# 48 constant products ahead of two projections of a hybrid decoder trunk

## The chip, the cores and the metric

The kernel runs on one core of a Trainium2 chip. The metric is the device time of one execution in microseconds (us). The engines are TensorE (PE, its weight loads PEld), VectorE (DVE), ScalarE (ACT), GpSimd (POOL) and SyncE (SP), which here only issues DMAs. Each engine works through its own queue in order and waits at the head of it on semaphores.

## The reference, cut to what matters

Two layers over 512 tokens of width 1024, float32. Layer 0 is a gated DeltaNet: one input projection gives queries, keys, values, a gate and two small sets of logits; a short causal convolution and SiLU follow; a delta rule in chunks runs over 16 value heads; a gated norm and an output projection end it. Layer 1 is a gated short convolution of width 2048.

```python
for i in range(DEPTH):
    h = rms_norm(x, pre_norm_w[i])
    if i % 2 == 0: y = gated_deltanet_mixer(h, ...)   # (h @ w_in) -> conv, SiLU, delta rule -> @ w_out
    else:          y = short_conv_mixer(h, ...)        # (h @ w_in) -> conv, gates -> @ w_out
    x = x + rms_norm(y, post_norm_w[i])
```

The change touches only TensorE's work around the first input projections of layer 0. Nothing that it computes goes into the result.

## The kernel before, in words

**Projections.** A projection of 128 output columns is a "unit": 1024 inputs are 8 blocks of 128, and each block takes three products of 128x128 by 128x512 in a float32 of reduced precision (`mm3`, lines 184 to 187: high by high, high by low, low by high). So a unit is 24 products into one PSUM bank. `unit` (line 189) first calls `weights` (line 172), which loads 512 KB of raw weights into `wraw`, casts them to a high part (line 167, on GpSimd for these units) and subtracts for the low part (line 168, on VectorE). `n_w` counts these calls. The high and low parts have two buffers each; once a tile `w3` exists, each call whose number divides by three puts its parts there instead (line 178, named `w` in the trace).

**Banks.** The units' banks come from the pool `ps_p`, which has two, both under the tag `pp`. A unit can begin when the unit two before it has been read out of its bank. For the first units of the kernel the read is one VectorE product with the row scales: line 363 (`start_keys`) for the four units of the start, which `start_unit` (line 868) emits, line 486 for the next four, which come from `in_unit` (line 479).

**The start.** The four units of the start are key 0, key 1, query 0 and query 1 of head group 0 (the first is computed beside the logits). Then come keys 0 and 1 and queries 0 and 1 of group 1: the calls of `unit` with `n_w` 1, 2, 3 and 4. In between stand small pieces of other work on TensorE. `norms` (line 540) transposes a key or query (tile `tok`) for ScalarE to square and sum (line 548, tile `junk`); `c_est` (line 561) follows it with the Gram products of a key (`kk`, line 583), the scaling of decay tables on ScalarE (line 597), and the products into `E` on VectorE (line 598). The triangular solve of a group (`c_solve`, line 611) starts from `E`: ScalarE copies at line 638, then a long run of small VectorE instructions at lines 645 and 647.

**What `w3` waits for.** `decay_tables` (line 422) for group 1 loads a table `gb` of 1 MB, applies 16 exponentials on ScalarE (line 449) and stores it by one DMA (line 454, `dt_d<-gb`). The tile `w3` has the same memory (tag `E3`, line 462), so the parts of the unit with `n_w` 3 can only be written when that DMA has read the table.

**Also at this time** the normed input is made for all later units: `start_h` (line 876) computes `hf` on VectorE (line 879) for 8 blocks, and splits each into `hh` (ScalarE, line 167) and `hl` (VectorE, line 168).

**What sets the order.** TensorE's order is that of the program text; other work is woven in by a counter of TensorE time that the text keeps itself (`pump.now`, advanced by `pump.pe`). VectorE's, ScalarE's and GpSimd's order is written out only up to line 890 (`start.close()`). After that, and for the DMA queue always, a planner in the compiler sets the order: it runs the program through a timeline of its own (line 38) and on each engine takes, of what is ready at that time, the instruction of the best priority. Priorities come from `pump.now` with an offset (`at`, line 149); weights and key norms have early ones, `start_h` late ones. So the planned order depends on when, in the planner's timeline, TensorE delivers.

**Constants.** `ones` (line 133) is a 128x128 float32 tile of ones. Fourteen products of it by itself stand at the very beginning (line 301).

Of the kernel before, what the change touches and what calls it, by code (L numbers as in the profile page):

```python
# [18 lines left out]
P = 128  # L19
# [41 lines left out]
}  # L61


class Pump:
# [46 lines left out]
def trunk_kernel(ctx, tc, xT, x, cols, rows, eye, post0, pre1, post1, w_in, w_out, sw_in, sw_out, out):  # L111
    nc = tc.nc
# [20 lines left out]
    ones = cst.tile([P, P], F32, name="ones")  # L133
# [3 lines left out]
                            fill=0.0, base=0, channel_multiplier=-1)  # L137
# [24 lines left out]
    def pd(shape, name):  # L162
        return ps_d.tile(shape, F32, tag="pd", name=name)
# [6 lines left out]
    third, n_w = [], [0]  # L170

    def weights(src, hi_eng=None, store=None):
# [8 lines left out]
        split(hi, lo, raw, hi_eng)  # L181
        return hi, lo

    def mm3(ps, lh, ll, rh, rl, start, stop):
        nc.tensor.matmul(ps, lhsT=lh, rhs=rh, start=start, stop=False)  # L185
        nc.tensor.matmul(ps, lhsT=lh, rhs=rl, start=False, stop=False)  # L186
        nc.tensor.matmul(ps, lhsT=ll, rhs=rh, start=False, stop=stop)  # L187

    def unit(src, rhs, t=slice(0, T), hi_eng=None):


        K, m, n = len(rhs), src.shape[2], t.stop - t.start
        with at(-20):
            hi, lo = weights(src, hi_eng)
        ps = ps_p.tile([P, n], F32, tag="pp", name="pp")
        for k in range(K):
            mm3(ps[:m], hi[:, k], lo[:, k], rhs[k][0][:, t], rhs[k][1][:, t], k == 0, k == K - 1)
            pump.pe(3 * MM * n / T)
        return ps
# [49 lines left out]
    with ExitStack() as L0:  # L249
# [33 lines left out]
        start = ExitStack()  # L283
# [253 lines left out]
                nc.scalar.activation(gs.zT[:, a], ps, AF.Silu)  # L537
            gs.nz += 1

        def norms(tl, ss):  # L540

            junk = dl.tile([P, P], F32, tag="junk", name="junk", bufs=1)
            tok = pd([P, NC, P], "tok")
            for c in range(NC):
                nc.tensor.transpose(out=tok[:, c], in_=tl[:, c * P:(c + 1) * P], identity=ident)
            pump.pe(0.43, False)
            for c in range(NC):
                last_sq = nc.scalar.activation(junk, tok[:, c], AF.Square, accum_out=ss[:, c:c + 1])
            nc.vector.tensor_scalar_add(ss, ss, EPS)
            return tok, last_sq  # L550

        def c_qnorm(gs, kh):
            while len(gs.kT) < 2 or gs.est <= kh:
                yield 0.5
            yield (15,)
            ss = sm.tile([P, NC], F32, tag="ssq", name="ssq")
            norms(gs.qT[kh], ss)
            nc.vector.tensor_scalar_mul(gs.epsa[:, kh], ss, EPS * P)
            gs.nq += 1

        def c_est(gs, kh):
            g = gs.g
            while not gates_done or (g > 1 and not groups[g - 2].done):
                yield 1
            kT = gs.kT[kh]
            if kh == 0:
                gs.nrm = dl.tile([P, 6, NC], F32, tag="nrm", name="nrm")[:, :2]
                gs.epsa = dl.tile([P, 2, NC], F32, tag="epsa", name="epsa")
                gs.bp, gs.bpe = (dl.tile([P, 4, NC], F32, tag=n, name=n) for n in ("bp", "bpe"))
                gs.E = dl.tile([P, 16, P], F32, tag="E", name="E", bufs=2)  # L570
            yield (11 if g else 4,)
            ss = sm.tile([P, NC], F32, tag="ssn", name="ssn")
            tok, last_sq = norms(kT, ss)
            ktok = dl.tile([P, NC, P], F32, tag="ktok", name="ktok", bufs=4)
            kte = 0 if g == 0 else 1
            if kte == 1:
                nc.scalar.copy(ktok, tok)
            gs.ktok[kh] = ktok
            normed_k.append(1)
            kk = pd([P, NC, P], "kk")  # L580
            for c in range(NC):
                s = slice(c * P, (c + 1) * P)
                nc.tensor.matmul(kk[:, c], lhsT=kT[:, s], rhs=kT[:, s], start=True, stop=True)
            pump.pe(0.9, False)
            rk2 = sm.tile([P, 1, NC], F32, tag="rk2", name="rk2")
            nc.vector.reciprocal(rk2[:, 0], ss)
            h2, g2 = slice(2 * kh, 2 * kh + 2), slice(4 * g + 2 * kh, 4 * g + 2 * kh + 2)
            nc.vector.tensor_tensor(out=gs.bp[:, h2], in0=beta[:, g2], in1=rk2.to_broadcast([P, 2, NC]), op=ALU.mult)
            for r in range(2):
                hl_, h = 2 * kh + r, 4 * g + 2 * kh + r  # L590
                if g == 0:
                    dt = dt0[h]
                else:
                    dt = es.tile([P, NC, P], F32, tag="dt", name="dt")
                    nc.sync.dma_start(out=dt, in_=dt_d[h])
                for c in range(NC):
                    nc.scalar.activation(dt[:, c], dt[:, c], AF.Copy, scale=gs.bp[:, hl_, c:c + 1])
                last_e = nc.vector.tensor_tensor(out=gs.E[:, 4 * hl_:4 * hl_ + 4], in0=kk, in1=dt, op=ALU.mult)
                nc.sync.dma_start(out=dt_d[h], in_=dt)
            if kte == 0:  # L600
                nc.vector.tensor_copy(ktok, tok)
            if g == 0:
                fence[:] = last_e, last_sq
            nc.vector.tensor_tensor(out=gs.bpe[:, h2], in0=gs.bp[:, h2], in1=edec[:, g2], op=ALU.mult)
            rk = rsqrt(sm, ss, [P, NC], "rk")
            nc.gpsimd.tensor_tensor(out=gs.nrm[:, kh], in0=ss, in1=rk, op=ALU.mult)  # L606
            gs.est += 1
            if gs.est == 2:
                pump.add(c_solve(gs))
# [193 lines left out]
        def c_gate(gs, c, po):  # L803

            g = gs.g
            s = slice(c * P, (c + 1) * P)
            junk = dl.tile([P, P], F32, tag="junk", name="junk", bufs=1)
            so = dl.tile([P, 4], F32, tag="so", name="so")
            for a in range(4):
                nc.scalar.activation(junk, po[:, a], AF.Square, accum_out=so[:, a:a + 1])  # L810
            fy = dl.tile([P, 4], F32, tag="fy", name="fy")
            nc.vector.scalar_tensor_tensor(out=fy.rearrange("p (k r) -> p k r", r=2),
                                           in0=so.rearrange("p (k r) -> p k r", r=2), scalar=1.0 / P,
                                           in1=gs.epsa[:, :, c:c + 1].to_broadcast([P, 2, 2]),
                                           op0=ALU.mult, op1=ALU.add)
            f = rsqrt(dl, fy, [P, 4], "f")
            while gs.nz < 4:
                yield 1
            of = dl.tile([P, 4, P], F32, tag="d3", name="of", bufs=2)
            for a in range(4):  # L820
                nc.scalar.activation(of[:, a], po[:, a], AF.Copy, scale=f[:, a:a + 1])
            po_live[0] -= 1
            yield (12,)
            pt = pd([P, 4, P], "pot")
            for a in range(4):
                nc.tensor.transpose(out=pt[:, a], in_=of[:, a], identity=ident)
            pump.pe(0.43, False)
            og = dl.tile([P, 4, P], F32, tag="d3", name="og", bufs=2)
            nc.vector.scalar_tensor_tensor(out=og, in0=pt, scalar=ccol(C_NW), in1=gs.zT[:, :, s],
                                           op0=ALU.mult, op1=ALU.mult)  # L830
            if g < 3:
                oh = dl.tile([P, 4, P], F32R, tag="d3", name="ohs", bufs=2)
                split(oh, og.bitcast(F32R), og)
                nc.sync.dma_start(out=og_d[0, g, :, :, s], in_=oh.bitcast(F32))
                nc.sync.dma_start(out=og_d[1, g, :, :, s], in_=og)
            else:
                if c == 0:
                    gs.oh = dl.tile([P, 4, T], F32R, tag="E", name="oh3", bufs=2)
                    gs.ol = dl.tile([P, 4, T], F32R, tag="zT", name="ol3")
                split(gs.oh[:, :, s], gs.ol[:, :, s], og)  # L840
            gs.ngate += 1
# [25 lines left out]

        def start_unit(w, kh, q, hooks={}):
            ps = ps_p.tile([P, T], F32, tag="pp", name="pp")
            for k in range(KD):  # L870
                mm3(ps, w[0][:, k], w[1][:, k], *xop[k], k == 0, k == KD - 1)
                pump.pe(3 * MM)
                hooks.get(k, lambda: None)()
            u_kq(first, kh, q, start_keys(ps))
# [58 lines left out]
        def out_products(h0, cs, n, hi_eng):  # L933

            banks = [ps_p.tile([P, 512], F32, tag="pp", name="pa") for _ in cs]
            for kk in range(4):
                with at(-16):
                    hi, lo = weights(w_out_v[:, h0 + 2 * kk:h0 + 2 * kk + 2, wide[n]], hi_eng)
# [250 lines left out]
```

## Time and profile before

| | us |
|---|---|
| time, median of 3 runs | 1017.25 |
| lowest and highest | 1015.12, 1018.17 |
| time of the profiled execution | 1017.51 |
| its span, first to last instruction | 1015.6 |
| TensorE busy within the span | 960.8 |
| VectorE, ScalarE, GpSimd busy | 611.7, 420.1, 239.6 |
| mean granted TensorE clock, share of full | 0.976 |

Times in the rows below count from the span's start. A row of the timeline gives start, length, engine, line, operation and tiles (output, then inputs), a count, and in brackets the idle time of the engine before it with what ended that. Matmul lengths are modelled and overlap, so the pace of a run is the distance between starts. A float32 product of `ones` leaves two matmul records. The granted clock is 1.00 at 2.4 GHz and 0.50 at 1.2 GHz.

### The profile page before, as it was taken

Reading aid. Unit: us, or ns where it says so; the run is one execution under the profiler, and the core shown is the slowest. Engines: PE = TensorE matmul, PEld = TensorE weight load, DVE = VectorE, ACT = ScalarE, POOL = GpSimd, SP = SyncE. Lnnn points to the kernel's source line nnn. Section 1 sums busy time; section 2 is a strip of 40 time slices with the busy share of each in tenths; the row PEclk is TensorE's granted clock in tenths of the full one; section 3 lists DMA queues with packets and bytes.
Section 4 is the critical chain, followed back from the end, with each engine's and each line's share of the span. In section 5 each row is a group of like instructions: output and inputs, shape, how many; then the busy total and the mean of one; then the engine's idle time right before and its main releaser. Section 6 shows DMA issues by size and latency. Waiting matters only on the chain.

```text
span 1015.6 us, 14732 instructions
## 1 busy us (share of the span) xinstructions
PE 960.8 (95%) x5430; PEld 805.5 (79%) x5430; DVE 611.7 (60%) x1100; ACT 420.1 (41%) x1002; POOL 239.6 (24%) x446
## 2 busy tenths in 40 slices
PE   7965989998999999999998899999999999999997
PEld 4854768886888788887876899888888888888886
DVE  8578998845996794735469976443344343342233
ACT  4576665535645644334212554233232233222123
POOL 6253731335235423416634000000000000000001
PEclk9886999999999999999999899999999999999999
DMA  6233763246334621793645566433333333323322
GB/s 195 70 110 125 228 199 116 62 137 175 104 88 152 179 81 53 225 354 126 206 135 178 150 174 181 131 93 104 93 94 104 94 93 104 94 92 104 97 91 83
DMA packets 172391, 133.91 MB, mean 132 GB/s; under 512 B 6272, under 2 KB 146176, under 8 KB 171936
## 3 DMA queue, kind: packets, MB, share of 16 engines
q1 hardware_dynamic: 172176, 132.88, 43.2%
q8 instruction: 43, 0.70, 0.3%
q14 instruction: 28, 0.23, 0.1%
q10 hardware_dynamic: 144, 0.09, 0.0%
HBM read 117.16 MB, written 15.79 MB: 131 GB/s over the span
## 4 chain that ended last, share of the span: by engine, by line
PE 70%; DVE 13%; DMA 7%; ACT 4%; issue 3%; POOL 3%; SPq 0%; POOLq 0%; DVEq 0%; ACTq 0%
PE pp L185 16%; PE pp L187 16%; PE pp L186 16%; PE pf L185 2%; PE pf L187 2%; PE pf L186 2%; DVE tm L645 2%; DVE wlo L168 2%; DMA eg<-gt_d 2%; DVE Na L647 2%; PE pa L186 1%; PE pa L187 1%; DMA gb<-gt_d 1%; PE pa L185 1%; PE u L759 1%
## 5 line engine op out<-in xcount | busy, mean ns | idle before, releaser
L185 PE MATMUL pp<-hh,whi 128*128 128x512 f32 (+1 forms) x624 | 236.7, 379 | 4.5 <-DVE acc L471 2.2
L186 PE MATMUL pp<-hl,whi 128*128 128x512 f32 (+1 forms) x624 | 231.0, 370 | 1.0 <-DVE r L988 1.0
L187 PE MATMUL pp<-hh,wlo 128*128 128x512 f32 (+1 forms) x624 | 231.0, 370 | 0.0
L168 DVE TENSOR_TENSOR wlo<-wraw,whi 128x1024 fp32r<-128x1024 f32 x115 | 141.8, 1233 | 134.0 <-ACT whi L167 107.3
L167 ACT CAST whi<-wraw 128x1024 fp32r<-128x1024 f32 x64 | 67.4, 1052 | 185.2 <-PE pp L186 107.4
L185 PEld LDWEIGHTS pp<-hh,whi 128*128 128x128 f32 x624 | 119.1, 191 | 24.2 <-POOL nrm L606 2.6
L187 PEld LDWEIGHTS pp<-hh,wlo 128*128 128x128 f32 x624 | 119.0, 191 | 20.0
L186 PEld LDWEIGHTS pp<-hl,whi 128*128 128x128 f32 x624 | 119.2, 191 | 19.0 <-DVE hl L168 1.2
L185 PE MATMUL pp<-hh,w 128*128 128x512 f32 (+1 forms) x304 | 114.9, 378 | 0.7 <-DVE acc L471 0.7
L187 PE MATMUL pp<-hh,w 128*128 128x512 f32 (+1 forms) x304 | 112.0, 368 | 1.3 <-DVE w L168 1.3
L186 PE MATMUL pp<-hl,w 128*128 128x512 f32 (+1 forms) x304 | 111.8, 368 | 0.0
L1145 POOL TENSOR_TENSOR ob<-ob,ytNa 128x384 f32<-128x384 f32 x2 | 2.1, 1038 | 450.0 <-ACT ob L1144 450.0
L167 POOL CAST whi<-wraw 128x1024 fp32r<-128x1024 f32 x51 | 65.4, 1283 | 84.7 <-PE pp L186 58.0
L168 DVE TENSOR_TENSOR w<-wraw,w 128x1024 fp32r<-128x1024 f32 x50 | 62.4, 1248 | 32.9 <-ACT w L167 30.7
L187 PEld LDWEIGHTS pp<-hh,w 128*128 128x128 f32 x304 | 57.5, 189 | 11.4 <-DVE w L168 1.8
L185 PEld LDWEIGHTS pp<-hh,w 128*128 128x128 f32 x304 | 57.7, 190 | 9.8 <-issue 1.1
L186 PEld LDWEIGHTS pp<-hl,w 128*128 128x128 f32 x304 | 57.7, 190 | 8.6
L471 DVE SCALAR_TENSOR_TENSOR acc<-pp,col,acc 128x511 f32<-128x511 f32 (+2 forms) x72 | 53.6, 744 | 13.2 <-ACT acc L468 12.3
L167 ACT CAST w<-wraw 128x1024 fp32r<-128x1024 f32 x25 | 26.3, 1052 | 66.2 <-PE pp L186 47.6
L647 DVE TENSOR_TENSOR Na<-Na,tm 128x126 f32<-128x126 f32 (+22 forms) x124 | 39.3, 317 | 2.7
L645 DVE TENSOR_TENSOR tm<-Na 128x126 f32<-128x126 f32 (+22 forms) x124 | 38.9, 314 | 2.9
L185 PE MATMUL pf<-whi,yh 128*128 128x512 f32 x104 | 40.5, 389 | 0.0
(310 smaller groups left out, 1726.0 us busy)
## 6 DMA issues: line engine op xcount, KB each, us to landing
wraw<-in_sw_in_dram SPq DMA_DIRECT2D x76, 512.0 KB, 3.9
wraw<-in_w_in_dram SPq DMA_DIRECT2D x47, 512.0 KB, 3.8
wraw<-in_w_out_dram SPq DMA_DIRECT2D x32, 512.0 KB, 4.2
wraw<-in_sw_out_dram SPq DMA_DIRECT2D x16, 512.0 KB, 3.5
eg<-gt_d SPq DMA_DIRECT2D x16, 256.0 KB, 4.3
dtq<-dt_d SPq DMA_DIRECT2D x16, 256.0 KB, 3.4
gb<-gt_d SPq DMA_DIRECT2D x3, 1024.0 KB, 6.8
dt_d<-gb SPq DMA_DIRECT2D x3, 1024.0 KB, 4.2
```

The lines of the kernel that those rows point to most:

```text
L167: (nc.scalar.copy if hi_eng is None else hi_eng.tensor_copy)(dst_hi, src)
L168: nc.vector.tensor_tensor(out=dst_lo, in0=src, in1=dst_hi.bitcast(F32), op=ALU.subtract)
L185: nc.tensor.matmul(ps, lhsT=lh, rhs=rh, start=start, stop=False)
L186: nc.tensor.matmul(ps, lhsT=lh, rhs=rl, start=False, stop=False)
L187: nc.tensor.matmul(ps, lhsT=ll, rhs=rh, start=False, stop=stop)
L471: nc.vector.scalar_tensor_tensor(out=acc[:, s:], in0=ps[:, :T - s], scalar=w(j), in1=acc[:, s:], op0=ALU.mult, op1=ALU.add)
L645: nc.vector.tensor_tensor(out=tv, in0=N[:, i:i + 1, 0:i].to_broadcast([P, w, i]), in1=X[:, m0:, i:i + 1].to_broadcast([P, w, i]), op=ALU.mult)
L647: nc.vector.tensor_tensor(out=X[:, m0:, 0:i], in0=X[:, m0:, 0:i], in1=tv, op=ALU.subtract)
L759: nc.tensor.matmul(u[:, a], lhsT=gs.E[:, 4 * a + c], rhs=X[:, a] if c else gs.nv[a][:, c], start=True, stop=True)
L1145: nc.gpsimd.tensor_tensor(out=ob[:, m], in0=ob[:, m], in1=yt[c][:, m], op=ALU.add)
```

## The change

A table says how many constant products to put where, and a helper puts them on TensorE: `ones` by `ones`, 128x128, each with its own start and stop, into the first 128 columns of the bank that the work after it begins anew. Only two entries are above zero: 20 products ahead of the unit with `n_w` 2, 28 ahead of the unit with `n_w` 3. The calls in `norms`, `c_gate`, `start_unit` and `out_products` find no entry and add nothing. `fill` does not advance `pump.now`.

```diff
+FILL = {"unit2": 20, "unit3": 28}
...
+    def fill(name, bank):
+        for _ in range(FILL.get(name, 0)):
+            nc.tensor.matmul(bank, lhsT=ones, rhs=ones, start=True, stop=True)
...
         ps = ps_p.tile([P, n], F32, tag="pp", name="pp")
+        fill("unit%d" % n_w[0], ps[:, :P])
         for k in range(K):
             mm3(ps[:m], hi[:, k], lo[:, k], rhs[k][0][:, t], rhs[k][1][:, t], k == 0, k == K - 1)
...
-        def norms(tl, ss):
+        def norms(tl, ss, name=""):
...
             tok = pd([P, NC, P], "tok")
+            fill(name, tok[:, 0])
```

## Rows read from the trace of the kernel before

**Rows 1.** Page, part 1: busy time, share of the span, instructions of each engine.
```profile
PE 960.8 (95%) x5430; PEld 805.5 (79%) x5430; DVE 611.7 (60%) x1100; ACT 420.1 (41%) x1002; POOL 239.6 (24%) x446
```
**Rows 2.** Timeline of TensorE, units n_w 1, 2, 3 and the first product of 4.
```profile
58.58 0.39 PE L187 MATMUL pp<-xh,wlo 128*128 128x512 f32 x1
65.30 0.76 PE L185 MATMUL pp<-xh,whi 128*128 128x512 f32 x1 [6.33 <-DVE pn L363]
...
70.43 0.40 PE L186 MATMUL pp<-xl,whi 128*128 128x512 f32 x1
...
72.03 0.39 PE L187 MATMUL pp<-xh,wlo 128*128 128x512 f32 x1
72.27 0.60 PE L545 MATMUL tok<-ident,kq 128*128 128x128 f32 x4
...
82.89 0.80 PE L185 MATMUL pp<-xh,w 128*128 128x512 f32 x1 [8.43 <-POOL w L167]
...
87.96 0.80 PE L187 MATMUL pp<-xh,w 128*128 128x512 f32 x1 [3.86 <-DVE w L168]
...
96.22 0.39 PE L185 MATMUL pp<-xh,whi 128*128 128x512 f32 x1
```
**Rows 3.** Timeline of VectorE: the reads that free the two banks.
```profile
64.47 0.68 DVE L363 TENSOR_TENSOR pn<-pp,bcs 128x512 f32<-128x512 f32 x1
65.07 0.68 DVE L486 TENSOR_TENSOR pn<-pp,bcs 128x512 f32<-128x512 f32 x1
```
**Rows 4.** Groups on TensorE, 0 to 42: busy us, mean ns of one, idle before.
```profile
L301 PE MATMUL wm<-ones 128*128 128x128 f32 x28 | 5.2, 369 | 1.1 <-DVE ones L134 1.1
...
L432 PE MATMUL pg<-utri,gg 128*128 128x128 f32 x32 | 3.8, 277 | 0.0
...
L369 PE MATMUL bc<-ident,rx 128*128 128x128 f32 x8 | 1.9, 420 | 0.0
```
**Rows 5.** Stretches: length, busy PE, PEld, DVE, ACT, POOL; clock, DMA share, GB/s.
```profile
65.30:69.80 4.50, 4.50 (x11) 3.53 (x12) 4.50 (x7) 2.50 (x5) 3.93 (x8) 0.50 0.43 138
69.80:74.46 4.66, 4.66 (x27) 3.67 (x25) 4.66 (x8) 1.53 (x8) 2.76 (x6) 1.00 0.35 97
74.46:82.89 8.43, 0.01 (x1) 0.01 (x1) 7.27 (x13) 6.52 (x11) 4.14 (x5) 0.63 0.32 125
...
87.96:93.69 5.73, 5.73 (x16) 4.56 (x17) 4.33 (x6) 3.84 (x11) 1.40 (x6) 0.50 0.62 183
```
**Rows 6.** Timeline of ScalarE, 56 to 92.
```profile
56.25 4.50 ACT L449 ACTIVATE gb<-gb,nG 128x128 f32<-128x128 f32 x15
...
66.68 1.12 ACT L167 CAST hh<-hf 128x512 fp32r<-128x512 f32 x2
72.90 0.28 ACT L548 ACTIVATE junk<-tok 128x128 f32<-128x128 f32 x1 [5.10 <-PE tok L545]
...
75.25 1.28 ACT L449 ACT_TABLE_LOAD   x1
76.54 0.40 ACT L449 ACTIVATE gb<-gb,nG 128x128 f32<-128x128 f32 x1
...
89.14 2.50 ACT L638 COPY Na<-E 32x512 f32<-32x512 f32 x4 [1.65 <-DVE E L598]
```
**Rows 7.** Timelines of the DMA queue, GpSimd and VectorE: the parts for n_w 3.
```profile
76.97 0.37 SPq L454 DMA_DIRECT2D dt_d<-gb  x1
...
81.30 1.53 POOL L167 CAST w<-wraw 128x1024 fp32r<-128x1024 f32 x1 [2.14 <-DMA dt_d<-gb]
...
86.70 1.21 DVE L168 TENSOR_TENSOR w<-wraw,w 128x1024 fp32r<-128x1024 f32 x1
```
**Rows 8.** Timeline of TensorE: the next wait after n_w 3.
```profile
107.53 1.13 PE L720 MATMUL kq<-kq 128*128 128x128 f32 x8 [1.87 <-DVE E L598]
```
**Rows 9.** Stretches as in rows 5, later.
```profile
90.00:140.00 50.00, 45.88 (x221) 37.71 (x220) 44.24 (x107) 31.77 (x102) 23.84 (x44) 0.96 0.61 187
...
600.00:700.00 100.00, 100.00 (x597) 89.49 (x596) 50.94 (x67) 37.68 (x53) 0.00 (x0) 1.00 0.47 134
```

More of the change, by code (lines that the diff above doesn't have):

```diff
@@ L556, in c_qnorm @@
             ss = sm.tile([P, NC], F32, tag="ssq", name="ssq")
-            norms(gs.qT[kh], ss)
+            norms(gs.qT[kh], ss, "qnorm%d%d" % (gs.g, kh))
             nc.vector.tensor_scalar_mul(gs.epsa[:, kh], ss, EPS * P)
@@ L572, in c_est @@
             ss = sm.tile([P, NC], F32, tag="ssn", name="ssn")
-            tok, last_sq = norms(kT, ss)
+            tok, last_sq = norms(kT, ss, "est%d%d" % (g, kh))
             ktok = dl.tile([P, NC, P], F32, tag="ktok", name="ktok", bufs=4)
@@ L824, in c_gate @@
             pt = pd([P, 4, P], "pot")
+            fill("pot%d%d" % (g, c), pt[:, 0])
             for a in range(4):
@@ L869, in start_unit @@
             ps = ps_p.tile([P, T], F32, tag="pp", name="pp")
+            fill("start%d%d" % (kh, q), ps[:, :P])
             for k in range(KD):
@@ L935, in out_products @@
             banks = [ps_p.tile([P, 512], F32, tag="pp", name="pa") for _ in cs]
+            fill("out%d" % n_w[0], banks[0][:, :P])
             for kk in range(4):
```

## The prediction

> **What bounds the kernel now.** The busy table comes first: TensorE is busy 95% of the span and no other engine over 60% [rows 1]. From 600 on it has no gap in a hundred us [rows 9]. So time that TensorE loses or wins early reaches the end, unless a wait on the way takes it up. The timeline of TensorE, read for idle time in brackets, shows the two longest waits and a third behind them [rows 2]: 6.33 us before the unit with n_w 2 (below: the second unit), which starts at 65.30; 8.43 us before the third, which starts at 82.89; and 3.86 us inside the third, after its first two products. The change puts 20 and 28 products into the first two.
>
> What each wait is for decides the rest. The second unit waits for line 363, which ends at 65.15 [rows 3]. That instruction reads the bank of the unit two before it: the second unit waits for its own bank. The third unit's bank was free at 65.75, when line 486 ended [rows 3]; it waits for its weights, first the high part (cast at 81.30, released by the store of the decay table), then the low part (86.70 to 87.91) [rows 7]. The store was issued at 76.97, because the last of 16 exponentials ran only at 76.54; fifteen were done by 60.75 [rows 6].
>
> The stretches show the clock [rows 5]: 0.50 from 65.30 to 69.80, 1.00 up to 74.46, 0.63 on average over the wait of 8.43 us, and 0.50 again from 87.96 to 93.69. After either wait the unit starts at 1.2 GHz.
>
> **The change part by part.** *Price of a fill.* Fourteen such products leave 28 records [rows 4], so 20 are 40 and 28 are 56. Thirty-two records of this size on the full clock are busy 3.8 us; less the 0.28 of the last, 3.52 / 31 = 0.113 us each. Eight on the low clock are busy 1.9; less 0.42, 1.48 / 7 = 0.211 each [rows 4].
>
> *First fill.* It writes the same bank, so it cannot start before line 363 has ended: it starts at 65.30, where the unit started, and not in the wait. The clock is low then and I let it rise 4.5 us after the start, as before [rows 5]. That is 21 records at 0.211 (4.5 us) and 19 at 0.113 (2.1 us): the fill ends at 71.9. The unit's 21 products up to the key norm then run at full pace, 0.228 us each (70.43 to 72.03 is 7 steps [rows 2]), 4.8 us: `tok` starts at 76.7 instead of 72.27, 4.4 later. The rest of the unit is as before (2.2 us) and ends at 78.9 instead of 74.46. Bounds for this edit alone: 0 if something else held the unit that long, +8.4 (40 x 0.211) if the clock stayed low through the fill, less the 2.2 us that the unit wins on the full clock (half of its slow 4.5).
>
> The Trainium skill bears on this place. "Perfetto Trace Analysis", section "Optimizing Tensor Performance: Matmuls", asks that independent groups of products rotate through different PSUM banks, so that the emptying of one overlaps with the products of the next. A fill in the bank that is being waited for is the contrary, and the trace agrees: no product stands in the 6.33 us. By that page's way, a fill in a spare bank would end before 65.30 and `tok` would come at 70.1, 2.2 earlier; by the row it comes 4.4 later.
>
> *Second fill.* Its bank is free, so it follows the second unit at once, at 78.9 and on the full clock: 56 x 0.113 = 6.3 us, to 85.2. Bounds: 6.3 at 2.4 GHz, 11.8 at 1.2 GHz. This lies wholly in the wait only if the weights of the third unit come after 85.2.
>
> *What the later `tok` does to the plan.* ScalarE was idle 5.10 us before squaring `tok` [rows 6]. In the planner's timeline it cannot have been idle there: the sixteenth exponential was ready (fifteen like it had run) and would have been taken. So the planner had `tok` ready when the second `hh` cast ended. With 40 records more on TensorE it has `tok` late, finds ScalarE free after that cast (67.8) and takes the sixteenth exponential, at about 67.8 + 1.28 of table load = 69.1. The third and fourth `hh` casts move ahead of the squares as well. The store then goes out near 69.5 and not 76.97; with 4.3 us to the cast as before (76.97 to 81.30) the high part starts at 73.8, and is done by 75.3; the low part can follow by 77 to 80, since it has an early priority. The third unit's weights are then there before the second fill has ended.
>
> *Sum.* The third unit starts at 85.2, on the full clock and without the wait of 3.86: 24 x 0.228 + 0.4 for the transposes in it = 5.9 us, end 91.2. Before it ended at 96.22 [rows 2]. That is -5.0. The solve's first copies came 16.9 us after `tok` (89.14 [rows 6]), and ScalarE spent part of that on the exponential, two table loads and `hh` casts, which now come before; I take the solve as unmoved, with bounds of 4 earlier and 4.4 later. Of the 5.0 I give 0.7 back at the next wait, 1.87 us for `E` on VectorE [rows 8], which is busy 44 of 50 us there [rows 9] and does not get all its work earlier (bounds 0 and 1.9, and up to 3 with smaller waits behind it). From the profiled execution's 1017.5, which is 0.3 from the median of 1017.25: 1017.5 - 5.0 + 0.7 = 1013.2.
>
> **The rivals.** *The planned order stays (slower).* If `tok` is not late in the planner's timeline, or the sixteenth exponential stays behind the squares, all that ScalarE does from 72.9 on is 4.4 us late: the store at 81.4, the high part at 85.7 to 87.2, the low part until 92.3. The second fill then ends inside the wait and hides, but 1.9 us of idle time, two products and a wait of 4.5 follow, so the clock is low again as at 87.96. The unit ends near 100.6: 1017.5 + 4.4 = 1021.9. It decides from the point where the store goes out after about 76. For it: the order before has this store so late, and the bank wait is in the trace. Against: ScalarE's idle 5.10 us, which such a planner does not leave.
>
> *VectorE holds the low part (no change).* The store moves, but the low part stays where it was in VectorE's queue, which is full at that time (7.27 of 8.43 us [rows 5]), until 87.9. The first two products run at 85.2, the other 22 and the transposes from 87.96 on the full clock, end 93.4: -2.8. If part of the queue before it comes late with `tok`, up to 4 us more: between 1014.7 and 1019, 1016.5 in the middle.
>
> *The change does what its words say.* Both fills lie in waits and the units run warm: `tok` at 70.1, 2.2 earlier, and half of the slow 5.73 us after 87.96 is won, 2.9: 1012.4. Against it stands line 363 ending 0.15 us before the second unit.
>
> **How the numbers follow.** A measurement of this kernel can tell about 0.3%, 3.05 us, from no change: faster is under 1014.2, slower over 1020.3. Forecast 0.48 (1010.5 to 1016), order kept 0.26 (1020 to 1023), VectorE 0.21, as its words say 0.05. Faster: 0.40 of the forecast and 0.04 of the last, 0.44. Slower: all of the order kept and 0.06 of the others, as a moved plan can lose later what it won: 0.32. The rest, 0.24, is within. The range takes both signs: 1010.5 (the forecast with the 1.87 us wait gone too and some luck) to 1022.5 (the order kept, 0.6 over). The likeliest case's own range is 1010.5 to 1016.
>
> **What the changed profile would show.** Right: 40 records on `ones` starting when line 363 ends, about 4.5 us of them at 0.50; `tok` near 76.7; the sixteenth exponential ahead of the squares and the store before 72; 56 records up to about 85, products of the third unit right behind them at 0.23 us, no wait for its low part, and the first product of the fourth unit near 91. Wrong: records on `ones` before 65; the store after 76; a wait inside the third unit; or TensorE ahead at 100 but level by 250, which would put the loss into a later plan.

## The result, and the profile after

The changed kernel takes 1027.96 us in the median of 4 runs (1025.82 to 1029.57); the kernel before, on the same chip, 1016.39 (4 runs, 1015.12 to 1018.17). The ratio is 1.0107, with an interval of [1.0087, 1.0127]: about 11 us slower. The forecast was 1013.2, the range ended at 1022.5. Lines of the changed kernel are 3 to 9 numbers higher in the rows shown here: L189 is the constant products, L192 to L194 the projections (185 to 187 before), L170 and L171 the high and low parts (167, 168).

The page of the changed kernel, part 1, answers to [rows 1]:

```profile
PE 973.5 (95%) x5526; PEld 818.0 (80%) x5526; DVE 612.3 (60%) x1100; ACT 421.4 (41%) x1002; POOL 228.4 (22%) x446
```

TensorE is busy 12.7 us longer, and the two fills, the groups of constant products, are 6.28 + 6.41 = 12.7 us. It is tempting to stop here (48 products added, their time lost). The timeline of TensorE forbids it; it answers to [rows 2]:

```profile
66.23 6.28 PE L189 MATMUL pp<-ones 128*128 128x128 f32 x40 [7.14 <-DVE pn L371]
...
77.17 0.60 PE L554 MATMUL tok<-ident,kq 128*128 128x128 f32 x4
...
79.20 6.41 PE L189 MATMUL pp<-ones 128*128 128x128 f32 x56
...
88.88 0.50 PE L192 MATMUL pp<-xh,w 128*128 128x512 f32 x1 [3.27 <-POOL w L170]
...
90.14 0.80 PE L194 MATMUL pp<-xh,w 128*128 128x512 f32 x1 [0.52 <-DVE w L171]
...
97.00 0.39 PE L194 MATMUL pp<-xh,w 128*128 128x512 f32 x1
97.22 0.39 PE L192 MATMUL pp<-xh,whi 128*128 128x512 f32 x1
```

The first fill does wait for the bank (7.14 us), and the second lies in a wait, of which 3.27 us are left behind it. The fourth unit, at 96.22 before, starts at 97.22. So with both fills spent, TensorE is only 1.0 us late. Matching TensorE's products of the two traces one by one (its order is the same in both) shows when the rest is lost: +1.2 us at 94.5, +1.0 at 97, +1.2 at 134.6, +2.0 at 240, then **+7.0 at 264**, +8.5 at 267, +10.9 at 353, +11.9 at the end (times of the changed kernel). The step lies 170 us behind the last added product. There, TensorE, ScalarE and VectorE in the changed kernel:

```profile
264.09 0.76 PE L192 MATMUL pp<-hh,whi 128*128 128x512 f32 x1 [4.62 <-DVE tm L654]
```

```profile
251.84 1.28 ACT L606 ACTIVATE dt<-dt,bp 128x128 f32<-128x128 f32 x4 [3.92 <-DMA dt<-dt_d]
...
256.07 2.52 ACT L647 COPY Na<-E 32x512 f32<-32x512 f32 x4 [0.23 <-DVE E L607]
258.61 0.69 ACT L476 ACTIVATE acc<-pp,col 128x512 f32<-128x512 f32 x1
```

```profile
258.62 2.02 DVE L648 STREAM_TRANSPOSE Na<-Na 128x1024 f32<-128x1024 f32 x1 [2.58 <-ACT Na L647]
260.55 0.73 DVE L479 SCALAR_TENSOR_TENSOR acc<-pp,col,acc 128x511 f32<-128x511 f32 x1
...
263.20 0.75 DVE L479 SCALAR_TENSOR_TENSOR acc<-pp,col,acc 128x509 f32<-128x509 f32 x1
```

and in the kernel before, ScalarE, VectorE and TensorE at the same place:

```profile
249.48 1.28 ACT L597 ACTIVATE dt<-dt,bp 128x128 f32<-128x128 f32 x4 [1.74 <-DVE wlo L168]
...
253.08 0.67 ACT L468 ACTIVATE acc<-pp,col 128x512 f32<-128x512 f32 x1
253.65 2.50 ACT L638 COPY Na<-E 32x512 f32<-32x512 f32 x4
```

```profile
253.79 2.31 DVE L471 SCALAR_TENSOR_TENSOR acc<-pp,col,acc 128x511 f32<-128x511 f32 x3 [0.41 <-ACT acc L468]
256.19 2.10 DVE L639 STREAM_TRANSPOSE Na<-Na 128x1024 f32<-128x1024 f32 x1
```

```profile
257.13 0.39 PE L185 MATMUL pp<-hh,whi 128*128 128x512 f32 x1
```

The unit at 257.13 needs a bank that four reads empty: the first convolution step on ScalarE (`acc`) and three on VectorE. Before, `acc` stood ahead of the four copies that open the triangular solve, the bank was free at 256.1, and TensorE did not wait. After, `acc` stands behind the copies, the transposition comes ahead of the three steps, and the bank is free at 263.95. The row names `tm` as what ended the wait; that is only the last VectorE instruction before it (263.87 to 264.05), and the bank's last read ends 0.1 us earlier. Behind the wait of 4.62 us the granted clock is also lower, 0.61 on average over 4.41 us, and TensorE loses another 1.5 us; the stretches before, in and behind it (length, busy PE, PEld, DVE, ACT, POOL; clock, DMA share, GB/s) are

```profile
250.00:258.00 8.00, 8.00 (x38) 6.60 (x37) 2.90 (x4) 5.87 (x17) 1.04 (x1) 1.00 0.40 119
258.00:264.09 6.09, 1.47 (x11) 1.01 (x9) 5.43 (x9) 3.51 (x12) 1.04 (x1) 1.00 0.71 206
264.09:268.50 4.41, 4.41 (x15) 3.62 (x16) 2.92 (x11) 2.89 (x14) 0.00 (x0) 0.61 0.36 102
```

A text comparison of the two programs' orders agrees: TensorE's is unchanged, but 85 rows of VectorE, 23 of ScalarE, 24 of GpSimd and 8 of the DMA queue stand elsewhere. A second, smaller loss stands behind 340 (+8.0 to +10.9). So the theory is that the planner's moved order costs most of the 11 us, and the fills' own time little. The rival is the plain one: the fills' TensorE time, first of all the 6 us behind the bank wait.

### The profile page after: what moved, and what is told of

Read it like the earlier page. It is cut to its first block, busy times and chain, and to the rows that moved or that the text cites. A ratio compares the mean times of both kernels' runs of the same rounds, so it can differ in the third digit from the quotient of the medians.

```text
span 1027.8 us, 14926 instructions
## 1 busy us (share of the span) xinstructions
PE 973.5 (95%) x5526; PEld 818.0 (80%) x5526; DVE 612.3 (60%) x1100; ACT 421.4 (41%) x1002; POOL 228.4 (22%) x446
## 4 chain that ended last, share of the span: by engine, by line
PE 74%; DVE 8%; DMA 6%; issue 4%; ACT 4%; POOL 3%; SPq 0%; POOLq 0%; DVEq 0%; ACTq 0%
PE pp L192 17%; PE pp L194 17%; PE pp L193 17%; PE pf L194 2%; PE pf L192 2%; PE pf L193 2%; PE pa L193 2%; PE pa L194 1%; PE u L768 1%; PE pa L192 1%; DMA wraw<-in_w_out_dram 1%; PE po L802 1%; DVE wlo L171 1%; DMA dtq<-dt_d 1%; PE psn L782 1%
## 5 line engine op out<-in xcount | busy, mean ns | idle before, releaser
L192 PE MATMUL pp<-hh,whi 128*128 128x512 f32 (+1 forms) x624 | 237.9, 381 | 10.7 <-DVE tm L654 4.6
L194 PE MATMUL pp<-hh,wlo 128*128 128x512 f32 (+1 forms) x624 | 231.7, 371 | 0.0
L171 DVE TENSOR_TENSOR wlo<-wraw,whi 128x1024 fp32r<-128x1024 f32 x115 | 142.7, 1241 | 137.0 <-ACT whi L170 107.9
L192 PEld LDWEIGHTS pp<-hh,whi 128*128 128x128 f32 x624 | 119.6, 192 | 30.5 <-issue 9.1
L170 ACT CAST whi<-wraw 128x1024 fp32r<-128x1024 f32 x64 | 67.4, 1052 | 184.8 <-PE pp L193 104.2
L194 PEld LDWEIGHTS pp<-hh,wlo 128*128 128x128 f32 x624 | 119.2, 191 | 20.4
L192 PE MATMUL pp<-hh,w 128*128 128x512 f32 (+1 forms) x304 | 114.9, 378 | 2.0 <-DVE rkt L217 0.9
L194 PE MATMUL pp<-hh,w 128*128 128x512 f32 (+1 forms) x304 | 111.9, 368 | 0.7 <-DVE w L171 0.7
L171 DVE TENSOR_TENSOR w<-wraw,w 128x1024 fp32r<-128x1024 f32 x50 | 62.6, 1253 | 32.5 <-ACT w L170 30.1
L170 POOL CAST whi<-wraw 128x1024 fp32r<-128x1024 f32 x51 | 57.6, 1130 | 102.6 <-PE pp L193 65.1
L192 PEld LDWEIGHTS pp<-hh,w 128*128 128x128 f32 x304 | 57.4, 189 | 11.6 <-issue 1.9
L194 PEld LDWEIGHTS pp<-hh,w 128*128 128x128 f32 x304 | 57.3, 189 | 10.8 <-DVE w L171 1.1
L170 ACT CAST w<-wraw 128x1024 fp32r<-128x1024 f32 x25 | 26.3, 1052 | 64.7 <-PE pp L193 46.4
L654 DVE TENSOR_TENSOR tm<-Na 128x126 f32<-128x126 f32 (+22 forms) x124 | 41.3, 333 | 2.8
L192 PE MATMUL pf<-whi,yh 128*128 128x512 f32 x104 | 40.5, 389 | 0.0
L193 PE MATMUL pf<-wlo,yh 128*128 128x512 f32 x104 | 40.5, 389 | 0.0
```

The lines of the kernel that those rows point to most:

```text
L170: (nc.scalar.copy if hi_eng is None else hi_eng.tensor_copy)(dst_hi, src)
L171: nc.vector.tensor_tensor(out=dst_lo, in0=src, in1=dst_hi.bitcast(F32), op=ALU.subtract)
L654: nc.vector.tensor_tensor(out=tv, in0=N[:, i:i + 1, 0:i].to_broadcast([P, w, i]), in1=X[:, m0:, i:i + 1].to_broadcast([P, w, i]), op=ALU.mult)
```

## The experiments

Ratios are against the kernel before on the same chip, with 95% intervals; they are not the ratio of the two medians, and differ from it by up to 0.2%. One chip's executions of the kernel before lie up to 10 us apart (1013.09 to 1022.61), and the trace of one can stand some 3 us off another in the same work (the run with one rule of order below is 2.9 us ahead before its rule acts), so that small differences of single traces are not read.

**The moved order without the fills.** The program is planned with all 48 products, and 45 of them are then taken out. Three carry semaphores and stay (the page counts 5436 records on TensorE, 6 more than before); the expectation counted four.

```diff
     with tile.TileContext(nc, **TC) as tc:      # FILL = {"unit2": 20, "unit3": 28}
         trunk_kernel(tc, *args)
+    remove_fill(nc)     # drops the products on ones into pp banks that wait for nothing and release nothing
```

> The program of the changed kernel, with the order that the planner gave it on all engines, but 44 of the 48 products are taken out of TensorE's queue after the planning (the first and last two of the pair of fills stay as far as they carry a wait or a count). Theory A (the plan): the 11 us come from the other order of VectorE, ScalarE, GpSimd and the DMA queue, which the planner made because its timeline has TensorE later; the products themselves cost little. It expects 1024 to 1029, and the large steps at about 257 and 340 of the span as in the changed kernel. Theory B (the products): TensorE's 12.7 us of products make the time. It expects 1015 to 1018.

Measured: 1025.3 us against 1017.72, ratio 1.0076 [1.0054, 1.0098]. TensorE is level at 94 us (-0.2), 1.2 us late at 152, and the step is where it was:

```profile
264.12 0.77 PE L185 MATMUL pp<-hh,whi 128*128 128x512 f32 x1 [5.36 <-DVE tm L645]
```

TensorE is 1.5 us late before that unit, 7.0 at its start and 9.7 behind it. The loss expected at about 340 is only 0.8 us here. Seven tenths of the loss (0.76% of 1.07%) come without the fills.

**The fills without the moved order.** The kernel before is planned as it is; then `insert_fill`, which edits the planned program, puts 20 and 28 products into TensorE's queue, in the units' own banks; the first of each waits for the bank as the unit does.

```diff
         trunk_kernel(tc, *args)                 # no FILL
+    insert_fill(nc, 2, 20)
+    insert_fill(nc, 3, 28)
```

> The kernel before with its own planned order on all engines; the 48 products are put into TensorE's queue after the planning, 20 and 28, into the same banks as in the change. Theory A expects no more than the local cost: TensorE late by up to 4.4 us at the second key norm and the third unit late by 0 to 4.4, so 1016 to 1021, and no step at 257. Theory B expects 1026 to 1029 as in the changed kernel.

Measured: 1021.76 us against 1017.72, ratio 1.0036 [1.0018, 1.0054]. TensorE's timeline:

```profile
65.78 6.21 PE L301 MATMUL pp<-ones 128*128 128x128 f32 x40 [7.04 <-DVE pn L363]
...
76.64 0.60 PE L545 MATMUL tok<-ident,kq 128*128 128x128 f32 x4
...
78.67 6.41 PE L301 MATMUL pp<-ones 128*128 128x128 f32 x56
...
87.26 0.50 PE L185 MATMUL pp<-xh,w 128*128 128x512 f32 x1 [2.18 <-POOL w L167]
...
92.34 0.80 PE L187 MATMUL pp<-xh,w 128*128 128x512 f32 x1 [4.34 <-DVE w L168]
```

TensorE is 4.4 us late when `tok` starts, 3.5 at 98, 3.9 at the end, and nothing happens at 257. This is the rival "the planned order stays", nearly to the row: it put the high part at 85.7 to 87.2, the low part at 92.3 and the sum at +4.4. The medians differ by 4.0.

**The second fill alone.** `FILL = {"unit3": 28}`; the order of every engine is then that of the kernel before.

> Only the 28 products ahead of the unit with n_w 3. The planned order of all engines is that of the kernel before. Theory A expects 1015 to 1017.5: the products lie in the wait, the clock stays up a little longer. Theory B in its form that each product costs its time: 1016.4 + 6.4 = 1022.8.

Measured: 1017.5 us against 1017.72, ratio 0.9991 [0.9975, 1.0008]. The stretches of the fill, of the rest of its wait, of the wait for the low part, and of the projection behind it (length, busy PE, PEld, DVE, ACT, POOL; clock, DMA share, GB/s):

```profile
74.08:80.49 6.41, 6.41 (x57) 6.22 (x55) 5.25 (x11) 6.35 (x13) 2.73 (x4) 1.00 0.44 167
80.49:82.68 2.19, 0.00 (x1) 0.00 (x1) 2.19 (x3) 0.35 (x1) 1.59 (x2) 1.00 0.00 0
82.68:87.79 5.11, 0.82 (x2) 0.30 (x3) 5.11 (x10) 4.05 (x11) 4.69 (x6) 0.55 0.65 205
87.79:93.50 5.71, 5.71 (x16) 4.57 (x17) 4.33 (x5) 3.82 (x11) 2.19 (x6) 0.51 0.66 184
```

It is wholly hidden, and it wins nothing that the interval shows: the clock holds through the fill and the next 2.19 us, and falls in the wait for the low part. The projection runs its sixteen slow products as before [rows 5].

**One product.** `FILL = {"unit2": 1}`.

> One single product ahead of the unit with n_w 2 and none ahead of the next: 0.4 us of TensorE time at most. The planner gives another order from there on (a few hundred places on four engines). Theory A expects a change of more than 3 us, in either direction, more likely slower. Theory B expects 1016 to 1017.

Measured: 1027.22 us against 1017.72, ratio 1.0086 [1.006, 1.0111], with one product of a few tenths of a us. VectorE has 101 rows elsewhere. The steps lie in other places: +7.4 us at 139, where TensorE waits

```profile
138.83 0.77 PE L185 MATMUL pp<-hh,w 128*128 128x512 f32 x1 [4.96 <-ACT zT L537]
```

and +9.1 at the end. A product of that length cannot cost 9 us by itself. What it shares with the change is that something was added ahead of the second unit; 28 products ahead of the third alone moved no row. So a fraction of a us ahead of that unit is enough for another order; why, no run shows.

**The first fill alone.** `FILL = {"unit2": 20}`, a third order (117 rows of VectorE, 21 of ScalarE).

> Only the 20 products ahead of n_w = 2, planned by the program as in the change. The order of TensorE is unchanged, that of the others is a third one (117 rows of VectorE lie elsewhere than in the kernel before, 85 in the changed kernel). Theory (the loss is the local 3.9 us or less plus whatever the moved order makes): ratio between 1.002 and 1.013, with steps at other places than 257 us. Rival (the loss at 257 us belongs to the later tok as such): the step of 7 to 8 us stands at 257 us here as well, and the ratio is 1.009 to 1.012.

Measured: 1021.09 us against 1016.49, ratio 1.0063 [1.0038, 1.0088]. No step at 257: `tok` is 4.2 us late here too, but TensorE is 1.2 us *ahead* at 257 and 1.4 late at the end of the profiled execution, the fastest of the six (1019.36 us; median 1021.09). The step does not belong to the later `tok` as such, then, but to one particular order. Where the median loses its 0.63% is not shown by this execution; the interval allows that it is all the local loss of the fill.

**That one order, and no product.** The kernel before with one rule: `acc` of column tile 22 comes behind the copies of the solve of head group 2.

```diff
...
-            nc.scalar.activation(acc, ps, AF.Copy, scale=w(3))
+            e = nc.scalar.activation(acc, ps, AF.Copy, scale=w(3)); ct == 22 and after(e, solved[2])
...
-                nc.scalar.copy(C[blk(b)], E[blk(b), :, blk(b)])
+                solved[gs.g] = nc.scalar.copy(C[blk(b)], E[blk(b), :, blk(b)])
```

> No product is added. To the kernel before one rule of order is added: on ScalarE the first copy that reads the bank of column tile 22 (the acc of the projection that TensorE begins at 244.9 us) comes behind the four copies that open the triangular solve of head group 2, as it does in the changed kernel; until about 253 us both kernels run the same orders. Theory (this one order makes the step at 257 us): the bank is freed only after the four copies (2.50 us) and the transposition on VectorE (2.3 us), so the projection that began at 257.1 us begins 3 to 7 us later, behind a product of the solve on VectorE, and the kernel takes 1020 to 1026 us, ratio 1.003 to 1.008. Rival (the step comes from the late loads of dt and the many other moved rows together): the projection begins within 1 us of 257.1 us and the ratio is 0.999 to 1.002.

Measured: 1023.37 us against 1016.49, ratio 1.0072 [1.0051, 1.0093], the size of the whole plan's loss. TensorE and ScalarE:

```profile
258.49 0.77 PE L185 MATMUL pp<-hh,whi 128*128 128x512 f32 x1 [4.13 <-DVE tm L645]
```

```profile
250.47 2.52 ACT L638 COPY Na<-E 32x512 f32<-32x512 f32 x4 [0.23 <-DVE E L598]
253.02 0.69 ACT L468 ACTIVATE acc<-pp,col 128x512 f32<-128x512 f32 x1
```

On VectorE the transposition comes ahead of the three reads of the bank here too, and the last of these ends at 258.35. This execution was 2.8 us ahead at 149; it is 1.4 late when that unit starts, 2.9 late at 261.6 (a step of 5.7), 7.1 late at 356 and 5.9 at the end. The planner also moves other work behind this place (61 rows of VectorE from here on), so the rule's whole consequence is shown, not that of two instructions alone. The rival, late loads of `dt`, falls: the step is here without them. In the changed kernel the scaling of `dt` starts 2.4 us later than before (251.84, 249.48), where TensorE is 2.2 us late anyway.

**The first fill in a bank that nobody waits for.** The order of the kernel before; 29 products ahead of the second unit go into the bank of the first products of the kernel (`wm`, line 299), which is free, and wait for nothing; 28 ahead of the third as before.

```diff
+    insert_fill(nc, 2, 29, spare=True)
+    insert_fill(nc, 3, 28)
```

> The order of all engines is that of the kernel before. Ahead of the projection n_w = 2 stand 29 products into a bank that nothing reads, so that they wait for nothing and lie inside the 6.33 us wait (29 x 0.227 us, the price of the fast records, are 6.6 us from 58.6 us on); ahead of n_w = 3 stand the same 28 products as before. Theory (the local loss of the change is the wait of its first products for the bank that the projection itself awaits): the +3.9 us of the kernel with the old order and both fills goes away, the projection starts at 65.3 to 65.6 us and runs at the fast clock, 1.0 to 1.4 us shorter; ratio 0.997 to 1.001. Rival (TensorE time as such costs, or the products disturb the other engines): ratio 1.003 to 1.006, as with the old order and both fills.

Measured: 1017.35 us against 1016.49, ratio 1.0013 [0.9998, 1.0028], a little over what the theory expected and under the rival's 1.003. No loss is shown any more, but no gain follows. TensorE:

```profile
59.36 6.64 PE L301 MATMUL wm<-ones 128*128 128x128 f32 x58
66.27 0.47 PE L185 MATMUL pp<-xh,whi 128*128 128x512 f32 x1 [0.27 <-DVE pn L363]
```

The unit runs at full pace from its start, `tok` comes at 71.12 (1.1 us earlier than before), and the third unit's low part starts at 88.18, where it did (87.96): it waits for its parts.

**The second fill up to the low part.** As the last, with 60 products ahead of the third unit.

> As the run with the spare bank, but 60 products instead of 28 ahead of n_w = 3: at 0.227 us they last 13.6 us, from some 73 us to some 87 us, past the moment at which the bits of the high part come (82.9 us) and up to the moment at which those of the low part come (88 us). Theory (28 products end too early, and the clock falls again before the projection gets going): the projection runs at the fast clock from 88 us on; its 16 products of the slow stretch 87.96 to 93.69 us take 16 x 0.227 = 3.6 us instead of 5.73 us, a gain of 2.1 us beside the 1.0 to 1.4 us of the spare bank; 1013 to 1015 us, ratio 0.996 to 0.998 if nothing is given back. Rival (the gain is given back at the next wait for another engine, as in the run of 28 products alone): ratio 0.999 to 1.001, and TensorE ahead at 96 us but level by 260 us.

Measured: 1017.26 us against 1016.49, ratio 1.0016 [0.9999, 1.0033], over the theory's 0.996 to 0.998 and nearer to the rival's. In the trace the two fills do what was hoped: the third unit runs on the fast clock and TensorE is 3.5 us ahead at 93.7. By 110.5 it is 0.3 late. The next wait, 1.87 us before [rows 8], is 3.23 us long, since the products `kq` that need `E` start only 2.1 us earlier. The stretches up to the wait, of the wait, and behind it, here:

```profile
90.30:102.20 11.90, 11.90 (x67) 9.94 (x65) 11.02 (x33) 5.97 (x24) 1.52 (x4) 1.00 0.16 47
102.20:105.44 3.24, 0.01 (x2) 0.03 (x1) 3.14 (x9) 3.21 (x13) 2.91 (x7) 0.82 0.86 278
105.44:110.50 5.06, 5.06 (x21) 4.77 (x22) 5.06 (x17) 2.14 (x11) 3.10 (x8) 0.50 0.73 188
```

and in the kernel before, of the wait and behind it:

```profile
105.44:107.53 2.09, 0.23 (x3) 0.03 (x1) 2.09 (x5) 2.06 (x10) 1.40 (x2) 1.00 0.65 251
107.53:110.50 2.97, 2.97 (x24) 2.84 (x24) 2.97 (x9) 1.61 (x9) 0.89 (x1) 1.00 0.84 221
```

An engine that comes early to a wait waits longer, and here the clock is 0.50 instead of 1.00 for the 5 us behind the longer wait. That the wait is the cause is put to the test next.

**A third fill in that wait.** As the last, with 14 products into the spare bank ahead of the products `kq`.

> As the run with the spare bank and the long second fill (there TensorE was 3.5 us ahead of the kernel before at 93.7 us, waited 3.23 us instead of 1.87 us for the product E of VectorE, ran the next 5.06 us at a granted clock of 0.50 and was 0.3 us behind at 110 us), with 14 more products into the spare bank in that wait, ahead of the products kq (L720), 14 x 0.227 = 3.2 us. Theory (the lead is lost because the longer wait lowers the clock): the clock stays at 1.00 from 105.4 to 110.5 us, and TensorE is 2 us ahead at 111 us; by 260 us 0 to 2 us of it are left, since three more waits for other engines follow; ratio 0.997 to 1.001. Rival (the lead is lost to the engine waited for, whatever the clock does): level or behind at 111 us with the clock at 1.00.

Measured: 1015.27 us against 1016.74, ratio 0.9982 [0.9966, 0.9998]; TensorE and stretches:

```profile
58.70 6.64 PE L301 MATMUL wm<-ones 128*128 128x128 f32 x58
...
71.98 13.56 PE L301 MATMUL pp<-ones 128*128 128x128 f32 x120
```

```profile
101.00:105.44 4.44, 4.34 (x37) 4.12 (x36) 4.37 (x12) 4.38 (x19) 3.33 (x7) 1.00 0.80 244
105.44:110.50 5.06, 5.06 (x30) 4.38 (x29) 4.97 (x21) 3.92 (x19) 3.90 (x12) 1.00 0.76 208
```

The clock holds at 1.00 and the lead survives: in this execution 4.9 us at 88.8, 3.5 behind the wait, 2.1 at 239, 2.5 at the end. With 103 products instead of 48, all in the order of the kernel before, the idea wins 1.5 us by the medians, and no more than 3.5 by the interval, which only just leaves out no change at all.

## Why the prediction was wrong

*Price of a fill*: right. 28 products took 6.41 us (forecast 6.3), 20 behind the bank wait 6.28 (6.6; the clock was 0.50 for the first 3.27 us, not 4.5).

*First fill*: right. It starts when VectorE's read of the bank ends (line 371, 363 before), not in the wait; `tok` came at 77.17 (76.7), and the unit ended at 79.20 (78.9). So the rival "the change does what its words say", with both fills inside waits, fell with the row at 66.23. For a spare bank the prediction put `tok` at 70.1; the runs with one had it at 69.95, 70.35 and 71.12. The Trainium skill ("Perfetto Trace Analysis", section "Optimizing Tensor Performance: Matmuls") asks that independent groups of products rotate through different banks; these three runs agree with it.

*Second fill*: right that it hides (ratio 0.9991 alone). That its wait would be over when it ends, with the unit right behind it, was wrong, and follows from the next step.

*What the later `tok` does to the plan*: this step failed. The third and fourth `hh` casts did move ahead of the squares, as forecast, but the sixteenth exponential stayed behind them:

```profile
77.81 0.28 ACT L557 ACTIVATE junk<-tok 128x128 f32<-128x128 f32 x1 [1.35 <-PE tok L554]
...
80.15 1.28 ACT L457 ACT_TABLE_LOAD   x1
81.44 0.40 ACT L457 ACTIVATE gb<-gb,nG 128x128 f32<-128x128 f32 x1
```

The store went out at 81.87, not near 69.5, and the high part came 14 us later than forecast (cast at 87.79, not 73.8). The argument was that a planner would not leave ScalarE idle for 5.10 us with an exponential ready; in the changed order ScalarE is again idle 4.95 and 1.35 us ahead of this exponential. What held it there in the planner's timeline is not in a trace of the chip, and stays open, as does why the new plan puts `acc` behind the copies at 257. The conclusion drawn from idle time on the chip about readiness in the planner's timeline was not warranted.

*Sum*: failed with it. The term "third unit starts at 85.2 on the fast clock, -5.0" measured +1.0 (fourth unit at 97.22 instead of 96.22). The unit started at 88.88, when the high part was there, and took 8.3 us instead of 5.9: the low part's first product came at 90.14, after a wait of 0.52 us (3.86 before), and then the clock was low, although a fill stood before it; 3.27 us of waiting lay between. The stretch, as in [rows 5]:

```profile
90.14:93.30 3.16, 3.16 (x8) 2.38 (x9) 0.55 (x1) 3.11 (x6) 1.39 (x8) 0.50 0.95 308
```

By 97 us 6 us of the miss had come (+1.0 for -5.0). The larger part, some 10 us behind it, is a term that the sum did not have. The sum priced a moved order by what it moves nearby, 0.7 us given back at the next wait, and took the rest as nothing; a loss on the other 900 us stood only in a chance of 0.06. The order was worth +0.76% [0.54, 0.98] alone, against +0.36% [0.18, 0.54] for the fills in the old order. That the two add up to 1.12%, beside 1.07% measured, is in part luck: at 97 us the fills make TensorE 3.5 us late in the old order but only about 1.2 in the new one (+1.0 with them, -0.2 without), where the low part comes at once. (85.2 and 5.9 also make 91.1 and not 91.2, which changes nothing.)

Of the rivals, "the planned order stays" had the local price right for the run in which the order did stay. It named this store (81.4 forecast, 81.87 measured) and the low clock in the third unit, but not the loss at 257, so its 1021.9 lay 6 us under the result. "VectorE holds the low part" fell: the low part followed the high one at once. Of the prediction's signs of being wrong two came, the store after 76 and a wait inside the third unit. The one that named a loss "into a later plan" was nearest to the rest, though TensorE was 1.0 us late at 97 and not ahead; no case of the sum carried that loss at its size.

## What to carry to other kernels

Where a planner orders the engines through a timeline of its own, an instruction added to one engine can be a new plan for all the others. Here one product ahead of the second unit moved 101 rows of VectorE and cost 0.86%, and 28 ahead of the third moved none: test it with one instruction, and compare orders before times. A filler that is to keep an engine warm (its clock high) must not share the resource that the engine waits for, must last until the work behind it can run, and must be followed to the next wait, where in this kernel the lead turned into a longer wait and a lower clock. Where TensorE is busy 95% of the span, look for a loss by matching its instructions one by one over the whole trace, not around the edit.

## What the hardware showed that was not expected

A wait of 1.87 us left the granted clock at 1.00 behind it (kernel before, 107.53), one of 3.23 us left it at 0.50 for at least 5.06 us (the run with 60 products): behind a wait 1.4 us longer, 2.4 us were lost by 110.5. With 14 constant products in that wait the clock stayed at 1.00. Products of constants kept the clock at 1.00 as well as real ones, in stretches up to 13.56 us long (the run with the third fill), and their price there was 0.226 us each (13.56 / 60).
